# Both ends of the state-space scan: where the decay products and the low parts of the scaled inputs run, when the last transposes come, and where the first branch operands lie

## The chip, the cores and the metric

The kernel runs on one core of one Trainium2 chip. The metric is the device time of one execution in microseconds, the median of repeated runs. Before the change it is 2060.22 us (three runs, 2060.09 to 2060.29). A core has TensorE (PE: matmuls, with its weight loads, PEld, beside them), VectorE (DVE), ScalarE (ACT), GpSimd (POOL) and the SyncE queue (SP), which here issues nearly all DMAs. Matmul results land in PSUM banks and are copied out by ScalarE or VectorE; operands lie in the on-chip memory SBUF.

## The reference

One layer of a hybrid encoder on 1024 frames of width 1024, in float32. Three mixers (latent attention, forgetting attention, a chunked state-space scan) read one input projection; their outputs are gated and merged, and a feed-forward block follows. What matters here is the scan and the merge:

```python
def ssd_scan(x, dt, A, Bm, Cm):
    ...
    a_cum = jnp.cumsum(dtc * A.astype(jnp.float32).reshape(G, Hg), axis=2)
    xdt = xf * dtc[..., None]
    ...
    decay = jnp.where(causal, jnp.exp(jnp.where(causal, seg, 0.0)), 0.0)
    cb = jnp.einsum('bcign,bcjgn->bcijg', Cc, Bc)
    y_diag = jnp.einsum('bcijg,bcijgh,bcjghp->bcighp', cb, decay, xdt)
    decay_to_end = jnp.exp(a_cum[:, :, -1:] - a_cum)
    states = jnp.einsum('bcjgn,bcjgh,bcjghp->bcghpn', Bc, decay_to_end, xdt)
    chunk_decay = jnp.exp(a_cum[:, :, -1])

    def step(h, inp):
        st, dec = inp
        return h * dec[..., None, None] + st, h
    ...
    y_off = jnp.einsum('bcign,bcghpn,bcigh->bcighp', Cc, h_in, jnp.exp(a_cum))
    return (y_diag + y_off).reshape(Bsz, L, H, P).astype(x.dtype)
...
        y_b = fox_branch(u_fox, fox_q_gain[l], fox_k_gain[l], fox_b_f[l]) @ w_br_fox[l]
...
        g = jax.nn.sigmoid(u_gate + b_gate[l]).reshape(Bsz, S, N_BRANCH, D_MODEL)
        merged = g[:, :, 0] * y_a + g[:, :, 1] * y_b + g[:, :, 2] * y_c
```

## The kernel before

Every float32 matmul is made of three on a reduced-precision type: an operand is **split** into a high part (a ScalarE copy) and a low part (a VectorE subtraction of the high part from the source), and high x high, high x low and low x high are summed (`mm3`, line 190; `split`, lines 136 and 137).

The stages run one after the other: input projection, attention of both kinds, scan, branch products with the gated merge, output product, feed-forward block. Projection blocks that nobody needs at once, twelve for the convolution and 24 for the gates (`all_fill`, matmuls at line 1153), are a **fill**: a generator that hands TensorE a few matmuls at a time between the work of attention and scan. In the scan one **step** of it is 12 matmuls of 512 columns; two steps make half a block, four a block. What follows a block (the tanh of a gate half at line 1160, the store of the gate to DRAM at line 1167, the split of the next weights at lines 1103 and 1104) is put in a queue with a due time on a running clock of estimated TensorE work (`later`, `run_until`).

The scan works on chunks of 128 rows, eight of them. Three generators serve a chunk, each one round after the other:

- `ssd_a` (round c): eight transposes of x in two groups into the one bank "tp" (lines 1484, 1485); then transposes of B and the products of B with C in the same bank (1493, 1495), the mask product cbm (1497), xd = x dt (1501) and its split into the two halves of xdt (136, 137), xdd and the skip term y on GpSimd (1504, 1506); then four times a decay matrix: a matmul "pse" into one of three "py" banks (1511), two ScalarE passes, the mask product, and a split into Eh and El.
- `ssd_b` (round c + 1): the states "pst" in one of two "st" banks (1534), the decayed state hst = previous hst x cdec (1539) plus pst (1540); four groups of output matmuls "py" (1548, 1549), each in a "py" bank which two VectorE additions into y free (1551, 1552); after the second group the product "pof" with the incoming state (1561 to 1564). At the end y is multiplied with silu of z (1567), Square on ScalarE sums its squares (1570) with the tile yT as a place for the squares nobody reads, GpSimd and VectorE take the inverse root in some ten small instructions, and ScalarE scales y (1575).
- `ssd_c` (round c + 2): eight transposes of y in two groups into "tp" (1583), copied to yT (1584), stored to ys_d in DRAM (1586).

The order on TensorE is that of the program in this stage. It is made by `merge`: of the streams of a round, always the one least far along (its cost so far over its estimate, from a start offset) is advanced to its next yield; the fill is a stream of its own with a budget per round (`FILL_SSD`). A stream that yields 0.0 lets the least advanced other stream go once. On the other engines a scheduler orders the instructions by estimated times. One that is pinned (`pin`, from line 1092 on `keep_in_program_order`) cannot go ahead of the instruction that the program has just before it on its engine; in this stage these are the splits of the gate weights and what follows a convolution block.

After round 9 the rest of the fill is run out and the branch stage starts: for forgetting attention, latent attention and the scan in turn, the branch outputs are loaded from DRAM (line 1626) into the four shared buffers "t4", split into ah and al (slots of one pool, eight each), and multiplied with the branch weights (loaded and split in `load_w`, line 1043); the result times the gate (loaded at 1645) goes into `merged` (1652). The memory of this stage lies where the scan's tiles lay; a tile waits until the tiles on whose place it lies have been read for the last time.

Of the kernel before, what the change touches and what calls it, by code (L numbers as in the profile page):

```python
# [21 lines left out]
P = 128  # L22
D = 1024
# [19 lines left out]
def block_kernel(ctx: ExitStack, tc: tile.TileContext, x, positions, norm_mix_g, w_in, b_gate,  # L43
# [85 lines left out]
    def uid(s):  # L129
        cnt[0] += 1  # L130
        return f"{s}_{cnt[0]}"
# [909 lines left out]
    def load_w(pool, src, nk=NK, he=None, le=None):  # L1041
        raw = pool.tile([P, nk, P], F32, name=uid("wr"), tag="wr")
        SY.dma_start(raw, src)
        h = pool.tile([P, nk, P], F32R, name=uid("wh"), tag="wh")
        l = pool.tile([P, nk, P], F32R, name=uid("wl"), tag="wl")
        split(h, l, raw, he, le)
        return h, l
# [87 lines left out]

    def all_fill():
# [5 lines left out]
        for n, (kind, j, c0) in enumerate(blocks):  # L1142
# [5 lines left out]
            for half in range(2):  # L1148
# [8 lines left out]
                if kind == "c":  # L1157
                    fn = lambda ps=ps, hs=hs, u=u: A.activation(u[:, hs], ps, AF.Copy)
                else:
                    fn = lambda ps=ps, hs=hs, u=u, r=8 * kind + j: A.activation(  # L1160
                        u[:, hs], ps, AF.Tanh, bias=pc_g[:, r:r + 1], scale=0.5)
                pl[0] = later(1.4, fn)
                if half == 1:
                    if kind == "c":
                        conv_done(j, u, ul, 2.2)
                    else:
                        ul[0] = later(2.0, lambda u=u, g=g_d[kind][j]: SY.dma_start(g, u))
# [268 lines left out]

    with ExitStack() as ps__:
# [37 lines left out]
        def ssd_a(o, c):  # L1475
# [5 lines left out]
            for g in range(2):  # L1481
# [4 lines left out]
                yield 0.44  # L1486
            if c + 1 < NT:
                load_xs(obj[c + 1], c + 1)
# [13 lines left out]
            split(o.xdt[:, :, 0:64], o.xdt[:, :, 64:128], xd)  # L1502
# [6 lines left out]
            for q in range(4):  # L1509
# [11 lines left out]
                o.E.append((Eh, El))  # L1521
                yield 0.3

        def ssd_b(o, c, prev):
# [4 lines left out]
            if c + 1 < NT:  # L1529
                o.hst = pool.tile([P, 16, 64], F32, name=uid("hst"), tag="hst")  # L1530
                for g in range(2):
# [6 lines left out]
                    else:  # L1538
                        V.tensor_mul(o.hst[:, hs, :], prev.hst[:, hs, :], hb(cdec, c, hs))
# [30 lines left out]
            A.activation(o.yT.rearrange("p j s -> p (j s)"), yf, AF.Square, accum_out=ss)  # L1570
# [4 lines left out]
            A.activation(yf, yf, AF.Copy, scale=r)  # L1575

        def ssd_c(o, c):

            yf = o.y.rearrange("p h d -> p (h d)")
            for g in range(2):  # L1580
# [4 lines left out]
                yield 0.44  # L1585
            SY.dma_start(ys_d[:, :, c * P:c * P + P].rearrange("j p s -> p j s"), o.yT)

        with tc.manual_schedule(engines={mybir.EngineType.PE}):
# [8 lines left out]
            for c in range(NT + 2):  # L1597
# [3 lines left out]
                if 0 <= c - 2 < NT:  # L1601
                    st.append((ssd_c(obj[c - 2], c - 2), 0.88, 0.6 if c <= NT else 0.9))
# [9 lines left out]
    with ExitStack() as pe_:  # L1612
        wsp = pe_.enter_context(TP("wsp", 1, side="right"))
        mgs = [pe_.enter_context(TP(f"mg{i}", 1)) for i in range(4)]
        mp_ = pe_.enter_context(TP("mgp", 1))
# [4 lines left out]
        run_until(clk[0] + 100.0)  # L1620
        mh, ml = alloc_hn()
        for b, wsrc, nk in ((1, w_br_fox, 4), (0, w_br_mla, 4), (2, w_br_ssm, 8)):
            ah, al = [], []
            for k in range(nk):
                raw = fpl.tile([P, S], F32, name=uid("ar"), tag="t4", bufs=4)
                SY.dma_start(raw, ys_d[k] if b == 2 else att_d[b][k * P:k * P + P, :])
                h = mp_.tile([P, S], F32R, name=uid("ah"), tag="ah", bufs=8)
                l = mp_.tile([P, S], F32R, name=uid("al"), tag="al", bufs=8)
# [4 lines left out]
                else:  # L1633
                    split(h, l, raw)
# [3 lines left out]
            for j in range(NK):  # L1638
                if (b, j) in ((0, 2), (0, 6), (2, 1), (2, 3), (2, 5)):
                    down_sums([wsp.tile([P, 2, 512], F32, name=uid("ws"), tag=f"ws{i}") for i in range(4)])  # L1640
                elif (b, j) == (2, 6):
                    down_flush()
                wh, wl = load_w(fpl, wv[:, :, j * P:j * P + P], nk)
                g = fpl.tile([P, S], F32, name=uid("gl"), tag="t4", bufs=4)
                SY.dma_start(g, g_d[b][j])
                for half in range(2):
# [9 lines left out]
                    if b == 2:  # L1656
# [4 lines left out]
                        if j == NK - 1 and half == 0:  # L1661
                            last = (i0, i1)
    psg.close()
# [68 lines left out]

    def behind_(ins, other):
        tc.add_manual_dep(ins.ins, other.ins.name,
                          mybir.DependencyInfo(mybir.DependencyClass.NoSync, mybir.DependencyReason.DATA),
                          reason="behind")
        return ins
# [408 lines left out]
```

## Time and profile before

| | us |
|---|---|
| median of the runs shown | 2060.22 |
| the profiled execution's own time | 2058.1 |
| its span, first to last instruction | 2056.4 |
| busy in the span: PE / DVE / ACT / POOL | 2017.6 / 1381.7 / 936.7 / 655.4 |
| scan stage in it, about | 919 to 1141 |
| branch stage in it, about | 1141 to 1321 |

How to read the rows: a list of waits gives engine and line, the engine and line waited for, the microseconds in total, the number of times, and the longest. A timeline row gives the start, the busy time, engine, line, operation, out <- in, partitions and shapes, the number of instructions merged into it, and in brackets the idle time ahead of it and what ended it. A window row gives the stretch, its length, busy time and number of instructions of PE, PEld, DVE, ACT and POOL, then the granted TensorE clock (1.00 is full), the share of the DMA engines, and GB/s. Ends of matmuls are modelled: a matmul's row reaches past the start of the next.

### The profile page before, as it was taken

Reading aid. Unit: us, or ns where it says so; the run is one execution under the profiler, and the core shown is the slowest. Engines: PE = TensorE matmul, PEld = TensorE weight load, DVE = VectorE, ACT = ScalarE, POOL = GpSimd, SP = SyncE. Lnnn points to the kernel's source line nnn. Section 1 sums busy time; section 2 is a strip of 40 time slices with the busy share of each in tenths; the row PEclk is TensorE's granted clock in tenths of the full one; section 3 lists DMA queues with packets and bytes.
Section 4 is the critical chain, followed back from the end, with each engine's and each line's share of the span. In section 5 each row is a group of like instructions: output and inputs, shape, how many; then the busy total and the mean of one; then the engine's idle time right before and its main releaser. Section 6 shows DMA issues by size and latency. Waiting matters only on the chain. (4 is left out here: it accounts for less than half of the span.)

```text
span 2056.4 us, 28859 instructions
## 1 busy us (share of the span) xinstructions
PE 2017.6 (98%) x10253; PEld 1681.5 (82%) x10253; DVE 1381.7 (67%) x2410; ACT 936.7 (46%) x1700; POOL 655.4 (32%) x638
## 2 busy tenths in 40 slices
PE   9999999999999999999999999999999999999999
PEld 8999888888888888887777787888778888888887
DVE  7777566366566766656776357557987777675655
ACT  5555323255454655545565223323545445454432
POOL 5033212122221322223332063000464454523765
PEclk9999999999999999999999999999999999999999
DMA  6266848343444545424433679432422211239575
GB/s 174 66 198 213 282 136 255 109 130 116 126 111 122 131 108 150 113 77 119 129 120 96 211 243 321 152 123 77 131 87 86 92 52 41 92 128 335 199 258 187
DMA packets 276315, 303.09 MB, mean 147 GB/s; under 512 B 19101, under 2 KB 209577, under 8 KB 276170
## 3 DMA queue, kind: packets, MB, share of 16 engines
q1 hardware_dynamic: 276168, 301.24, 46.9%
q8 instruction: 81, 1.33, 0.3%
q14 instruction: 64, 0.52, 0.1%
q10 hardware_dynamic: 2, 0.00, 0.0%
HBM read 208.51 MB, written 92.67 MB: 146 GB/s over the span
## 5 line engine op out<-in xcount | busy, mean ns | idle before, releaser
L1297 POOL TENSOR_SCALAR pm<-pm,rs 128x128 f32<-128x128 f32 (+7 forms) x128 | 107.1, 840 | 426.7 <-DVE rs L1296 320.7
L1153 PE MATMUL mm<-hnh,wh 128*128 128x512 f32 x576 | 240.2, 417 | 0.0
L1153 PE MATMUL mm<-hnh,wl 128*128 128x512 f32 x576 | 226.6, 393 | 0.0
L1153 PE MATMUL mm<-hnl,wh 128*128 128x512 f32 x576 | 226.6, 393 | 0.0
L2093 PE MATMUL dn<-dr,dr 128*128 128x512 f32 x592 | 182.3, 389 | 0.0
L1290 ACT ACTIVATE pm<-s,nmx 128x128 f32<-128x128 f32 (+2 forms) x192 | 110.3, 581 | 71.3 <-DVE nmx L1287 61.3
L2093 PEld LDWEIGHTS dn<-dr,dr 128*128 128x128 f32 x592 | 111.1, 188 | 23.0
L1153 PEld LDWEIGHTS mm<-hnh,wl 128*128 128x128 f32 x576 | 108.6, 189 | 24.7
L1153 PEld LDWEIGHTS mm<-hnh,wh 128*128 128x128 f32 x576 | 109.4, 190 | 19.9 <-issue 4.4
L1153 PEld LDWEIGHTS mm<-hnl,wh 128*128 128x128 f32 x576 | 109.4, 190 | 15.9 <-issue 0.5
L1357 DVE TENSOR_TENSOR ptl<-tp,pth 128x512 fp32r<-128x512 f32 (+1 forms) x160 | 97.9, 631 | 34.0 <-ACT pth L1356 32.6
L2093 PE MATMUL dn<-dr 128*128 128x512 f32 x296 | 115.3, 389 | 1.1 <-DVE dY L2110 1.1
L1356 ACT ACTIVATE pth<-tp 128x512 fp32r<-128x512 f32 (+1 forms) x160 | 83.9, 555 | 69.3 <-PE tp L1351 69.2
L137 DVE TENSOR_TENSOR dr<-dr,dr 128x1024 fp32r<-128x1024 f32 x52 | 72.2, 1398 | 52.1 <-ACT dr L136 39.5
L190 PE MATMUL ybr<-ah,wh 128*128 128x512 f32 x256 | 100.1, 395 | 3.1 <-ACT ah L136 1.6
L190 PE MATMUL ybr<-al,wh 128*128 128x512 f32 x256 | 99.8, 392 | 0.2
L190 PE MATMUL ybr<-ah,wl 128*128 128x512 f32 x256 | 99.2, 390 | 0.0
L1285 DVE TENSOR_REDUCE nmx<-s 128x1 f32<-128x384 f32 (+3 forms) x128 | 65.9, 519 | 35.9 <-PE s L1284 34.5
L136 ACT ACTIVATE dr<-dr 128x1024 fp32r<-128x1024 f32 x52 | 54.9, 1063 | 72.9 <-PE dn L2093 51.2
L136 ACT ACTIVATE wh<-wr 128x1024 fp32r<-128x1024 f32 (+1 forms) x40 | 35.2, 879 | 101.3 <-PE ybr L190 53.1
L1351 PE MATMUL tp<-ident,pm 128*128 128x128 f32 x576 | 80.5, 275 | 0.0
L137 DVE TENSOR_TENSOR wl<-S,wh 128x1024 fp32r<-128x1024 f32 x42 | 63.2, 1504 | 23.5 <-ACT wh L136 23.5
(529 smaller groups left out, 5882.3 us busy)
## 6 DMA issues: line engine op xcount, KB each, us to landing
dr<-act_d SPq DMA_DIRECT2D x99, 256.0 KB
wr<-in_w_in_dram SPq DMA_DIRECT2D x36, 512.0 KB
g_d<-t SPq DMA_DIRECT2D x24, 512.0 KB
gl<-g_d SPq DMA_DIRECT2D x24, 512.0 KB
wr<-in_ffn_w_up_dram SPq DMA_DIRECT2D x23, 512.0 KB
ws<-in_ffn_w_down_dram SPq DMA_DIRECT2D x22, 512.0 KB
wsum_d<-ws SPq DMA_DIRECT2D x22, 512.0 KB
act_d<-fa SPq DMA_DIRECT2D x22, 512.0 KB
```

Source lines behind the costliest of these rows:

```text
L136: i = A.activation(h, src, AF.Copy) if he is A else he.tensor_copy(h, src)
L137: return i, le.tensor_sub(l, src, f32(h))
L190: T.matmul(ps, a(k), b(k), start=(i == 0), stop=(i == n - 1))
L1153: T.matmul(ps, a[:, k, :], b[half][:, k, :], start=(k == 0 and i == 0), stop=(k == NK - 1 and i == 2))
L1285: later(0.15, lambda: V.reduce_max(nmx[:, ci:ci + 1], ps[:, :b - a], axis=AX, negate=True))
L1290: pss[cj][1][0] = later(0.9 + 0.1 * cj, lambda cj=cj, a_=a_, b_=b_: A.activation(p_[:, a_:b_], pss[cj][0][:, :b_ - a_], AF.Exp, bias=nb, a ...
L1297: G.tensor_scalar(p_[:, 0:n * P], p_[:, 0:n * P], rs[:, 3:4], 0.0, op0=ALU.mult, op1=ALU.add)
L1351: T.transpose(pt[:, off:off + P], pn[qi][0][:, k * P:k * P + P], ident)
L1356: later(cs + 0.05, lambda th=th, pt=pt, off=off: A.activation(th[:, :off], pt[:, :off], AF.Copy))
L1357: pl[0] = later(cs + 0.6, lambda th=th, tl=tl, pt=pt, off=off: V.tensor_sub(tl[:, :off], pt[:, :off], f32(th[:, :off])))
L2093: T.matmul(ps[m], a[:, ts_], b[:, 512:], start=first_ and j == 0 and q == 0, stop=j == NFH - 1 and q == 2, skip_group_check=not first_)
```

## The change

Seven edits, all around the scan:

1. The decay product of `ssd_b` (line 1539) is pinned: it stays behind the VectorE instruction that the program has just before it.
2. The split of xd leaves its place behind xd: the high part is issued behind the first decay block of the round, the low part, pinned, behind the second.
3. `ssd_a` gets an empty yield between the second group of x transposes and the transposes of B; `ssd_c` one behind its first group, except in the last chunk.
4. Square writes to a scratch tile of its own, ysq (4 KB a partition), in place of yT.
5. In round 9 the stream of `ssd_c` gets cost 8.0 and offset 0.2 in place of 0.88 and 0.9. The tanh of the very last gate half and the store behind it are due 50 us later.
6. The first two fox outputs are loaded into a pool of their own, opened ahead of the scan on the other side of memory (two of the four scratch tiles of the down sums move there as well). The operand pairs of fox are four fixed pairs of tiles, high and low in turn, ahead of the others in memory.
7. On ScalarE, the high parts of fox's operands and of its first weight block are ordered behind the last scale of y (1575), and the last gate tanh and the second weight block behind the second high part.

```diff
+    def behind_(ins, other):
+        tc.add_manual_dep(ins.ins, other.ins.name,
+                          mybir.DependencyInfo(mybir.DependencyClass.NoSync, mybir.DependencyReason.DATA),
+                          reason="behind")
+        return ins
+
+    def load_w(pool, src, nk=NK, behind=None):
...
-        split(h, l, raw, he, le)
+        i, _ = split(h, l, raw)
+        if behind is not None:
+            behind_(i, behind)
...
+    def gate_tanh(o, i, b):
+        t = A.activation(o, i, AF.Tanh, bias=b, scale=0.5)
+        if gate_behind[0] is not None:
+            behind_(t, gate_behind[0])
...
-                pl[0] = later(1.4, fn)
+                wait = 50.0 if n == len(blocks) - 1 and half == 1 else 0.0
+                pl[0] = later(wait + 1.4, fn)
...
+    pfr = ExitStack()
+    frp = pfr.enter_context(TP("frp", 1, side="right"))
...
                 A.activation(xT[:, 512 * g:512 * g + 512], pt, AF.Copy)
                 yield 0.44
+            yield 0.0
...
             V.tensor_mul(xd, xv, hb(dt, c))
-            split(o.xdt[:, :, 0:64], o.xdt[:, :, 64:128], xd)
...
                 o.E.append((Eh, El))
+                if q == 0:
+                    A.activation(o.xdt[:, :, 0:64], xd, AF.Copy)
+                elif q == 1:
+                    pin(V.tensor_sub(o.xdt[:, :, 64:128], xd, f32(o.xdt[:, :, 0:64])))
                 yield 0.3
...
-                        V.tensor_mul(o.hst[:, hs, :], prev.hst[:, hs, :], hb(cdec, c, hs))
+                        pin(V.tensor_mul(o.hst[:, hs, :], prev.hst[:, hs, :], hb(cdec, c, hs)))
...
-            A.activation(o.yT.rearrange("p j s -> p (j s)"), yf, AF.Square, accum_out=ss)
+            sq = pool.tile([P, D], F32, name=uid("ysq"), tag="ysq", bufs=1)
+            A.activation(sq, yf, AF.Square, accum_out=ss)
...
-            A.activation(yf, yf, AF.Copy, scale=r)
+            scaled[0] = A.activation(yf, yf, AF.Copy, scale=r)
...
                 yield 0.44
+                if g == 0 and c + 1 < NT:
+                    yield 0.0
...
-                    st.append((ssd_c(obj[c - 2], c - 2), 0.88, 0.6 if c <= NT else 0.9))
+                    st.append((ssd_c(obj[c - 2], c - 2), *((0.88, 0.6) if c <= NT else (8.0, 0.2))))
...
-        mp_ = pe_.enter_context(TP("mgp", 1))
+        mps = [pe_.enter_context(TP(n, 1)) for n in ("mpf", "mpm")]
...
-        run_until(clk[0] + 100.0)
...
+        def ops_tile(i):
+            return [mps[i // 4].tile([P, S], F32R, name=uid(n), tag=f"{n}{i}") for n in ("ah", "al")]
...
+                if b == 1 and k < 2:
+                    raw = frp.tile([P, 2, 512], F32, name=uid("ar"), tag=f"ws{k}").rearrange("p a s -> p (a s)")
+                else:
+                    raw = fpl.tile([P, S], F32, name=uid("ar"), tag="t4", bufs=4)
...
-                    split(h, l, raw)
+                    e = split(h, l, raw)
+                    if b == 1:
+                        behind_(e[0], scaled[0])
+                        if k == 1:
+                            gate_behind[0] = e[0]
+                            run_until(clk[0] + 100.0)
...
-                wh, wl = load_w(fpl, wv[:, :, j * P:j * P + P], nk)
+                wh, wl = load_w(fpl, wv[:, :, j * P:j * P + P], nk, (scaled, gate_behind)[j][0] if b == 1 and j < 2 else None)
```

26 lines of the change are left out of this document (13 added, 13 removed).

## The prediction

> **What bounds the kernel now.** I read the page first, then TensorE's waits in the stretch that the diff touches, then the timeline of each engine around every wait, and last the windows with the granted clock.
>
> ```profile
> span 2056.4 us, 28859 instructions
> ...
> PE 2017.6 (98%) x10253; PEld 1681.5 (82%) x10253; DVE 1381.7 (67%) x2410; ACT 936.7 (46%) x1700; POOL 655.4 (32%) x638
> ```
>
> TensorE is the bound from end to end. The change adds and removes no matmul, so it can only win TensorE's idle time, and whatever slower clock follows an idle stretch. Between 905 and 1150 us, the scan and the head of the branch stage, these are all of its waits over 0.5 us but the one at the scan's door, which nothing in the diff reaches:
>
> ```profile
> PE py L1548 <- DVE y L1552: 2.9, 1, 2.9
> PE stp L1493 <- ACT xT L1485: 2.1, 3, 0.7
> PE ybr L190 <- ACT ah L136: 1.6, 1, 1.6
> PE stp L1583 <- ACT yT L1584: 1.1, 1, 1.1
> PE stp L1583 <- ACT y L1575: 1.1, 1, 1.1
> ```
>
> Together 8.8 us, in four places. The first and the third cost more than they show. TensorE's timeline after the 2.9, then the windows there and at the end:
>
> ```profile
> 950.35 0.32 PE L1548 MATMUL py<-xdt,Eh 128*128 128x128 f32 x1 [2.90 <-DVE y L1552]
> ...
> 953.36 0.63 PE L1153 MATMUL mm<-hnl,wh 128*128 128x512 f32 x1
> 953.79 0.63 PE L1153 MATMUL mm<-hnh,wl 128*128 128x512 f32 x1
> ...
> 957.20 0.44 PE L1153 MATMUL mm<-hnl,wh 128*128 128x512 f32 x1
> ```
> ```profile
> 948.00:954.00 6.00, 3.65 (x12) 2.99 (x13) 4.08 (x8) 2.36 (x5) 0.00 (x0) 0.71 0.01 1
> 954.00:960.00 6.00, 6.00 (x22) 4.30 (x22) 2.61 (x5) 3.34 (x7) 0.00 (x0) 0.72 0.11 40
> 960.00:966.00 6.00, 6.00 (x29) 4.89 (x28) 4.68 (x9) 4.81 (x9) 2.18 (x5) 1.00 0.75 228
> ...
> 1140.00:1146.00 6.00, 4.39 (x12) 3.55 (x13) 1.56 (x2) 3.44 (x4) 0.00 (x0) 0.72 0.99 291
> ```
>
> The granted clock (the figure after POOL's) is 0.71 and 0.72 behind those two stalls and 1.00 elsewhere. From 950.35 to 957.20 the 512-wide matmuls start 0.43 us apart; at full clock it is 0.23 (1137.37 to 1137.60 in the end's rows below). A slow stretch so loses 0.20/0.43 of its length: 6.85 x 0.47 = 3.2 us here. The start stall costs 2.9 + 3.2 = 6.1.
>
> **Part 1, the start.** Who is late for that matmul: it needs the third "py" bank, which VectorE frees with two additions. VectorE's rows, the last of an undisturbed xd product:
>
> ```profile
> 940.00 1.29 DVE L1537 COPY hst<-pst 128x512 f32<-128x512 f32 x2
> 941.20 3.02 DVE L1539 TENSOR_TENSOR hst<-hst,cdec 128x512 f32<-128x512 f32 x2
> 944.14 2.92 DVE L1501 TENSOR_TENSOR xd<-xT,dt 128x1024 f32<-128x1024 f32 x1
> ...
> 948.19 1.23 DVE L137 TENSOR_TENSOR xdt<-xd,xdt 128x1024 fp32r<-128x1024 f32 x1 [0.79 <-ACT xdt L136]
> ...
> 949.78 0.42 DVE L1552 TENSOR_TENSOR y<-y,py 128x256 f32<-128x256 f32 x1
> ...
> 969.59 1.23 DVE L1501 TENSOR_TENSOR xd<-xT,dt 128x1024 f32<-128x1024 f32 x1 [1.26 <-ACT xT L1485]
> ```
>
> Two things stand ahead of the additions and are not wanted yet: the decay products of chunk 1 (3.02), floated one round early, and the low part of xdt (0.79 wait and 1.23), which the next round's matmuls read. The pin sends the first back to its own round (two instructions of about 0.65, beside pst), behind the VectorE instruction issued just ahead of it in the program; the move sends the second behind the second exponential block. Then xd can start when the transposed x is there, about 941.7, and ends at 944.6 even at its disturbed 2.92; the small cbm product (0.41) and the first two additions (0.87) follow. The third py falls at about 946.3 in the new order of part 2 (from 940.39: four transposes 0.36, a gate step 2.7, B's 0.6, two py groups 0.9 each, one pse 0.4), with the first py done at 945.2, so the additions end about 946.1. That is tight: any 0.4 to 0.7 us instruction in the way shows. I take 5.8 of the 6.1; bounds 0 (still over 2 us late) and 6.1. What moves in elsewhere: 1.3 us of products at each round's start, against 1.2 to 2 us of low part leaving that place, on a VectorE that is busy 4.68 us of the window 960 to 966. That is the slower rival's ground.
>
> **Part 2, the empty yield.** I worked the rule of the merge (always the stream least far along) through both versions, with 44 gate steps of 12 matmuls left (the first of 6) and -0.1 us owed at the start, which reproduces the order of the trace in all ten rounds. In rounds 1, 4 and 7 nothing stands between the second x transposes and those of B, which wait for the one transpose bank:
>
> ```profile
> 940.39 0.60 PE L1484 MATMUL stp<-ident,t 128*128 128x128 f32 x4
> 941.68 0.44 PE L1493 MATMUL stp<-ident,bc 128*128 128x128 f32 x2 [0.69 <-ACT xT L1485]
> ```
>
> With the yield a gate step (2.7) or a py group (0.9) comes between in every round: 3 x 0.69 = 2.1 us. The cover is longer than the 0.69 it hides. B's transposes, and the mask product and exponentials behind them, come later by as much; their readers stand in the next round, over 6 us on. Bounds 0 and 2.1; taken 2.1.
>
> **Part 3, Square in its own tile.** In round 3 and at the end ScalarE's Square waits until the previous chunk's store has read yT:
>
> ```profile
> 989.80 1.06 ACT L1570 ACTIVATE yT<-y 128x1024 f32<-128x1024 f32 x1 [2.60 <-DMA ys_d<-yT]
> 1001.43 1.15 ACT L1575 ACTIVATE y<-y,yr 128x1024 f32<-128x1024 f32 x1 [4.03 <-POOL yr L182]
> ```
>
> The scale of the same chunk comes 11.6 us later, and the transposes at 1002.6 wait 1.1 us for it. 2.6 us earlier covers that: 1.1, bounds 0 and 1.1.
>
> **Part 4, the end.**
>
> ```profile
> 1120.65 0.48 PE L1153 MATMUL mm<-hnh,wh 128*128 128x512 f32 x1
> ...
> 1137.37 0.39 PE L1153 MATMUL mm<-hnh,wl 128*128 128x512 f32 x1
> 1137.60 0.60 PE L1583 MATMUL stp<-ident,y 128*128 128x128 f32 x4
> 1139.32 0.65 PE L1583 MATMUL stp<-ident,y 128*128 128x128 f32 x4 [1.12 <-ACT yT L1584]
> 1141.61 2.07 PE L190 MATMUL ybr<-ah,wh 128*128 128x512 f32 x4 [1.63 <-ACT ah L136]
> ...
> 1145.12 0.40 PE L190 MATMUL ybr<-ah,wl 128*128 128x512 f32 x1
> ```
> ```profile
> 1121.76 1.22 DVE L1567 SCALAR_TENSOR_TENSOR y<-y,t 128x1024 f32<-128x1024 f32 x1
> ...
> 1145.67 3.50 DVE L137 TENSOR_TENSOR al<-ar,ah 128x1024 fp32r<-128x1024 f32 x3 [2.86 <-DMA ys_d<-yT]
> ```
> ```profile
> 1124.77 0.36 SPq L1586 DMA_DIRECT2D ys_d<-yT  x1
> ...
> 1128.83 2.49 SPq L1626 DMA_DIRECT2D ar<-att_d  x3
> ```
> ```profile
> 1128.06 1.06 ACT L1570 ACTIVATE yT<-y 128x1024 f32<-128x1024 f32 x1 [0.16 <-DVE wl L137]
> ...
> 1132.42 1.15 ACT L1575 ACTIVATE y<-y,yr 128x1024 f32<-128x1024 f32 x1 [3.21 <-POOL yr L182]
> ...
> 1140.51 2.94 ACT L136 ACTIVATE ah<-ar 128x1024 fp32r<-128x1024 f32 x3
> ```
>
> Now the last transposes, their copies and the first fox split stand in a row with nothing beside them: 1.12 + 1.63 = 2.75 us idle, then a slow clock to 1145.12: 3.51 x 0.47 = 1.65. In the new order the six gate steps from 1120.65 (72 matmuls, 2.7 each) run: two, second transposes of chunk 6, two, first transposes of chunk 7, one, second transposes of chunk 7, one. The first transposes of chunk 7 thus fall near 1131.9. Is y scaled by then? Its product ends at 1122.98; Square then waits for the store issued at 1124.77 and for what is queued ahead, and the scale ends 5.5 us after Square starts (1128.06 to 1133.58). In its own tile Square can start at 1123, so the scale ends near 1128.6, 3.3 us before it is wanted. Behind it stand the two first fox high parts (about 1.0 each), then their low parts (1.23); 2 x 2.2 us fits ahead of the last gate step's end near 1138. Both copies of the transposes lie under the last two gate steps. The last tanh goes behind the second high part; nobody waits for it but its store. Six loads are touched: two raw loads leave SP's 1128.83 group for memory of their own, two keep the shared buffers, and two weight loads only have their splits ordered. The low part that waited 2.86 for the store lay on yT's place; by the sizes of the tiles the four fox pairs now lie below it, on xdt, xd, xdd and y, read out by then, save the fourth low part, which waits for chunk 7's transposes. Taken 4.4; bounds 0 and 4.4.
>
> **The sum.** 5.8 + 2.1 + 1.1 + 4.4 = 13.4. The idle figures count from a matmul's modelled end, 0.16 past the next one's start (0.39 long, 0.23 apart), so each of seven bridged stalls gives 0.15 more: 1.0. In all 14.4. Against the profiled span that is 2056.4 - 14.4 = 2042.0, against that execution's own 2058.1 it is 2043.7, and against the median of the runs shown, 2060.2, it is **2045.8**. In the rest of the branch stage, to 1330, TensorE's longest wait is
>
> ```profile
> PE ybr L190 <- ACT ah L1630: 1.2, 1, 1.2
> ```
>
> so that stage has no slack in which the gain could drown, and behind it TensorE stays the bound.
>
> [...]
>
> **The rivals.**
> - Start stall stays (0.10): VectorE runs another floating instruction ahead of the additions, which no pin forbids. For it: the 0.2 us margin. Gives back 5.8 and 0.2: 2051.8.
> - The end turns into a new wait (0.13): Square does not come forward, because ScalarE's order puts a weight copy that waits for TensorE ahead of it; the scale then ends at 1133.6, and TensorE stands 1.7 us at 1131.9 and hardly less ahead of ybr. Against it: those copies are now ordered behind the scale. About 3 us less: 2049.
> - The slow stretches are no consequence of the stalls (0.04): 3.2 + 1.65 stay: 2050.6. The rows speak against it, both standing directly behind a stall.
> - No effect (0.04): VectorE is late in any order, or the two halves cancel: 2060.
> - **Slower (0.09):** the VectorE instruction just ahead of the pinned decay products is, from round 2 on, the second seed of the previous chunk's inverse root, which waits for Square and GpSimd:
>
> ```profile
> 991.26 0.15 DVE L175 TENSOR_SCALAR rg_i<-yv 128x1 int32<-128x1 int32 x1 [3.29 <-POOL yv L1572]
> ```
>
>   The products, the additions of pst that free the "st" banks, and whatever else VectorE has queued then stand behind that wait, and TensorE at pof in each of rounds 2 to 7. A stall like the one at 950 costs 6.1; two leave a gain, from the third it is slower, six give 2060.2 - 14.4 + 36.6 = 2082. Against it: pof follows pst by two py groups and at least one gate step, some 5 us, against 2.6 us for products and additions, and Square comes earlier where it was held up.
>
> **How the numbers follow.** The forecast has 0.60. Below 2043.5 nothing is left to win but the scan's door. Up to 2053 the range holds the first three rivals: about 0.82 in all after the edges of each. What cannot be told from no change is 0.2%, 4.1 us. Faster: 0.60 + 0.10 + 0.13 + 0.04 = 0.87; same 0.04; slower 0.09.
>
> **What would show it.** Right: no 2.9 us wait at py L1548 and a clock of 1.00 around it; the decay products in 2 x 0.65 beside pst from round 2 on; no wait of B's transposes for xT; Square with no wait for ys_d; both last transposes before the last gate matmuls, and ybr directly behind these at full clock. Wrong: a wait at py, pof or the y transposes that was not there, above all one longer than 2 us with slow matmuls behind it.

## The result, and the profile after

The changed kernel takes 2047.38 us (median of 6 executions, 2045.54 to 2048.7) beside 2060.2 us of the kernel before on the same chip (6 executions); ratio 0.9938, 95% interval 0.9925 to 0.9951. The profiled execution took 2045.89 us, its span is 2044.2, 12.2 less than before. The forecast was 2045.8, with 14.4 less.

The page of the changed kernel, its first lines:

```profile
span 2044.2 us, 28874 instructions
...
PE 2013.8 (99%) x10253; PEld 1678.3 (82%) x10253; DVE 1387.1 (68%) x2410; ACT 936.4 (46%) x1700; POOL 652.9 (32%) x638
```

TensorE's waits in the changed kernel, as far as they belong to the scan and the branch stage (engine and line, what was waited for, us in total, times, longest):

```profile
PE stp L1502 <- DVE o L1349: 0.9, 1, 0.9
...
PE ybr L190 <- ACT ah L1665: 0.7, 1, 0.7
PE ybr L190 <- DVE al L1666: 0.7, 1, 0.7
PE stp L1502 <- ACT yT L1607: 0.6, 2, 0.3
...
PE stp L1606 <- ACT y L1598: 0.2, 1, 0.2
```

None of the five waits that the prediction listed is left in its size: the 2.9 of the third output group, the three of 0.69 and the 1.6 ahead of ybr are gone, and of the waits of the y transposes 0.2 is left. The 0.9 is the one at the scan's door. The two rows of ybr stand far behind the head of the branch stage, at 1222 and 1226 us, where the scan's own outputs come in; before waits 1.2 us at that place. Now the stretch in which the 2.9 stood, first as windows (length, then busy time and number for PE, PEld, DVE, ACT, POOL, then the granted clock), then as TensorE's timeline:

```profile
942.00:948.00 6.00, 6.00 (x41) 5.25 (x39) 3.47 (x8) 2.49 (x4) 4.88 (x2) 0.98 0.34 88
948.00:954.00 6.00, 6.00 (x14) 3.94 (x14) 4.36 (x7) 2.56 (x5) 0.00 (x0) 0.50 0.02 3
954.00:960.00 6.00, 6.00 (x29) 4.64 (x30) 3.88 (x7) 4.69 (x8) 0.00 (x0) 0.95 0.43 146
```
```profile
944.46 0.31 PE L1570 MATMUL py<-xdt,Eh 128*128 128x128 f32 x1
...
947.76 0.79 PE L1529 MATMUL pse<-segr,segl 10*128 10x512 f32 x1
948.49 0.80 PE L1168 MATMUL mm<-hnh,wh 128*128 128x512 f32 x1
...
953.90 0.79 PE L1529 MATMUL pse<-segr,segl 10*128 10x512 f32 x1
954.62 0.33 PE L1570 MATMUL py<-xdt,Eh 128*128 128x128 f32 x1
```

TensorE is busy for all of the 18 us, there is no stall, and still the clock is 0.50 from 947.76 to 954.62. This is the surprise of the result: the stall went and the half clock behind it stayed, 6.86 us long as before (6.85). At the end of the scan it did go. The same views there, and ScalarE's timeline:

```profile
1128.00:1134.00 6.00, 6.00 (x30) 4.91 (x29) 2.36 (x2) 3.85 (x5) 0.00 (x0) 1.00 0.75 274
```
```profile
1126.03 0.60 PE L1606 MATMUL stp<-ident,y 128*128 128x128 f32 x4
1129.24 0.60 PE L1606 MATMUL stp<-ident,y 128*128 128x128 f32 x4
1132.45 0.62 PE L190 MATMUL ybr<-ah,wh 128*128 128x512 f32 x2
```
```profile
1116.89 1.06 ACT L1593 ACTIVATE ysq<-y 128x1024 f32<-128x1024 f32 x1 [2.39 <-DVE y L1589]
...
1121.35 1.15 ACT L1598 ACTIVATE y<-y,yr 128x1024 f32<-128x1024 f32 x1
...
1130.37 2.00 ACT L136 ACTIVATE ah<-ar 128x1024 fp32r<-128x1024 f32 x2
```

Square waits for its product and no longer for a store; the scale ends at 1122.5, 3.5 us ahead of the first of the last transposes; both groups of these have gate matmuls behind them, and the first branch matmul follows the last gate matmul without a gap.

### The profile page after: what moved, and what is told of

The parts are those of the page before. It is cut to its first block, busy times and chain, and to the rows that moved or that the text cites. A ratio compares the mean times of both kernels' runs of the same rounds, so it can differ in the third digit from the quotient of the medians.

```text
span 2044.2 us, 28874 instructions
## 1 busy us (share of the span) xinstructions
PE 2013.8 (99%) x10253; PEld 1678.3 (82%) x10253; DVE 1387.1 (68%) x2410; ACT 936.4 (46%) x1700; POOL 652.9 (32%) x638
```

## Where the 12.2 us come from

The two timelines give three lengths: from the first x transposes (919.30 before, 920.01 after) to the first branch matmul (1141.61, 1132.45), from there to the last branch matmul, and the rest.

| | before | after | won |
|---|---|---|---|
| ahead of the scan | 919.30 | 920.01 | -0.7 |
| scan, first x transposes to first ybr | 222.31 | 212.44 | 9.9 |
| branch matmuls | 178.52 | 176.82 | 1.7 |
| the rest of the span | 736.3 | 734.9 | 1.3 |

The first row lies outside of the diff, and of the last row the diff touches only where two scratch tiles lie. Both move from profile to profile where no edit reaches: in the fourteen profiles of this study the scan begins anywhere between 919.30 and 927.01, and in the thirteen of the changed kernel and its variants the rest goes from 734.4 to 736.4, so that before's 736.3 lies within. That is more than most of the edits are worth, so below a kernel is judged by the length of its scan and by the waits in it, beside its median.

| kernel | median us | ratio to before, 95% | scan us | half-clock windows in it |
|---|---|---|---|---|
| before | | | 222.31 | 2 |
| after | 2047.38 | 0.9925 to 0.9951 | 212.44 | 2 |
| again | 2046.55 | 0.9924 to 0.9952 | 210.88 | 1 |
| broken_run | 2045.46 | 0.9917 to 0.9945 | 211.17 | 1 |
| second_run | 2049.02 | 0.9934 to 0.9969 | 210.07 | 0 |
| fine_steps | 2047.52 | 0.9928 to 0.9957 | 211.34 | 0 |
| fine_round1 | 2046.33 | 0.9924 to 0.9951 | 209.33 | 0 |
| no_pin | 2051.45 | 0.9939 to 0.9974 | 214.67 | 2 |
| low_part_early | 2047.34 | 0.9925 to 0.9958 | 213.35 | 2 |
| no_yield | 2049.35 | 0.9935 to 0.9969 | 214.08 | 1 |
| square_yT | 2054.99 | 0.9970 to 0.9991 | 218.02 | 2 |
| late_transposes | 2051.65 | 0.9946 to 0.9974 | 213.58 | 1 |
| free_order | 2053.01 | 0.9953 to 0.9977 | 211.47 | 0 |
| old_memory | 2046.30 | 0.9925 to 0.9953 | 209.30 | 0 |

A half-clock window is explained next. All kernels but before are the changed kernel with the edit shown. From again on they ran in three groups, each on a chip of its own beside executions of before, whose medians were 2059.37, 2060.03 and 2059.82; so medians of different groups can be compared to within about 0.7 us.

## Experiments on the clock

**again**: no edit.

> The changed kernel itself, timed again beside the three below. Theory 'light windows': the clock of TensorE is decided window by window, each about 3.4 us long, on a grid that is not tied to the program, and a window with little matmul work in it (idle, or 128-column matmuls with fresh weights) halves it for the next one or two. Then the three groups of output matmuls in a row in round 1 are hit in some executions and missed in others: mean clocks between 0.998 and 1.000, spans that differ by 1.6 to 3.4 us between them, median near 2047. Rival 'the place': the clock falls whenever the scan starts; every execution shows 0.998 and they lie within 1 us.

Its six executions have mean clocks from 0.998 to 1.000, spans from 2042.2 to 2046.8 and a median of 2046.55. "The place" falls. In its profile the clock is halved only from 950.8 to 954.2, in a scan of 210.88 us; in the changed kernel's first profile it was halved for twice as long, in a scan of 212.44. The instructions are the same, and nothing in round 1 waits in either.

**Where half clock begins.** The windows of 0.2 us in which it sets in, of before, of broken_run and of second_run:

```profile
544.20:544.40 0.20, 0.00 (x0) 0.00 (x0) 0.20 (x2) 0.00 (x0) 0.00 (x0) 0.73 0.58 205
950.40:950.60 0.20, 0.20 (x2) 0.20 (x3) 0.17 (x2) 0.00 (x0) 0.00 (x0) 0.70 0.00 0
1141.60:1141.80 0.20, 0.20 (x1) 0.20 (x2) 0.20 (x1) 0.20 (x1) 0.00 (x0) 0.56 1.08 328
```
```profile
545.80:546.00 0.20, 0.20 (x4) 0.20 (x3) 0.20 (x2) 0.20 (x1) 0.00 (x0) 0.75 1.15 266
955.40:955.60 0.20, 0.20 (x3) 0.15 (x2) 0.20 (x2) 0.20 (x1) 0.00 (x0) 0.75 0.00 0
```
```profile
39.80:40.00 0.20, 0.20 (x3) 0.20 (x2) 0.20 (x2) 0.20 (x2) 0.15 (x1) 0.51 0.96 389
821.40:821.60 0.20, 0.20 (x3) 0.20 (x3) 0.20 (x2) 0.00 (x0) 0.00 (x0) 0.64 1.00 410
```

A mean of 0.73 over 0.2 us that begin at 1.00 and end at 0.50 puts the edge at 0.46 of the way, 544.29. So the edges lie at 544.29, 950.48 and 1141.62 in before, at 545.90 and 955.50 in broken_run, at 39.80 and 821.46 in second_run. Their distances, 406.19, 191.14, 409.60 and 781.66, are 119, 56, 120 and 229 times 3.4133, each within 0.02 us. The unit is measured: the clock record of before's trace has half-clock stretches of 3.413, 6.827 and 3.413 us, that of the changed kernel one of 6.827 (the 6.86 above is counted between starts of matmuls), and the four distances divided by their counts give 3.4132 to 3.4134. Every half-clock stretch of these profiles that the end of the span doesn't cut is one or two such lengths long. So in these profiles half clock begins on a grid of 3.413 us which the program's start doesn't place: counted back by 159 lengths, an edge lies at 1.6 us of before's span (544.29 - 542.7) and at 3.2 of broken_run's (545.90 - 542.7). A length of the grid at half clock costs 1.6 us: 212.44 (two) - 210.88 (one).

What comes ahead of the edges at the scan's start is a length of the grid in which TensorE does little. In the changed kernel it is 944.35 to 947.76: B's last products, three output groups and a decay matmul, without any wait. The output groups bring 192 columns in 0.22 us, where the gate matmuls bring 512 in 0.23; by that the window holds about two fifths of the columns of a gate window (an estimate from these spacings). In before it is 947.07 to 950.48, of which the stall takes 2.9.

So in the changed kernel a length that was busy throughout, with narrow matmuls, was enough for half clock: PE busy 3.41 of the 3.41 us from 944.35 to 947.76, then 0.50 in the window from 948 to 954 above.

**broken_run** moves one gate step of round 1 ahead of the third output group:

```diff
-    FILL_SSD = [11.3] * 8 + [12.0, 24.5]
+    FILL_SSD = [11.3, 11.9, 10.7] + [11.3] * 5 + [12.0, 24.5]
```

> One gate step is moved ahead of the third output group of round 1, so that no three output groups stand in a row there. 'Light windows': no clock under 0.98 between 935 and 965, mean clock 0.999 to 1.000 in nearly every execution, about 2 us less than 'again' in the median and up to 3.2 less where that one was hit. 'The place': a slow stretch of 3.4 or 6.8 us stays at the scan's start, time within 0.5 us of 'again'.

A miss in the profile: half clock from 955.50 on, for one length of the grid. The gate step ends at 951.44, and from there to 954.96 come the third output group, two decay matmuls, the fourth group and another decay matmul, with 0.45 us of wait for an exponential. The light stretch was cut at one place and made at the next, and half clock moved with it. The mean clock of its six executions is 0.9995 beside 0.9986 of the changed kernel's twelve, and the medians are not told apart.

**second_run** gives round 4 the order of round 1:

```diff
-                if q == 1 and prev is not None:
+                if q == (3 if c == 3 else 1) and prev is not None:
```

> The product with the incoming state of chunk 3 comes after the fourth output group in place of after the second, so that round 4 has the order of round 1: B's transposes, two output groups, a decay matmul, the third output group, a decay matmul, a gate step. 'Light windows': a second slow stretch of 3.4 or 6.8 us near 1015 to 1035 in a good part of the executions, mean clocks down to 0.996, median 1 to 3 us above 'again'. 'The place': no slow clock there, time within 0.7 us of 'again' (the banks of the moved product may cost some tenths).

Its profile shows neither: no half clock in the scan at all, though now two rounds have the three groups. The edges of its grid, counted on from 821.46, fall at 1016.02, 1019.43 and 1022.84; the light stretch of round 4, from 1016.74 to 1021.46, lies across the middle one, and neither side was light enough, a wait of 0.33 us for an exponential included. Other executions do pay, by their clocks: two of its six have a mean clock of 0.996, where none of the changed kernel's twelve is under 0.998, and the median is 2.5 us over again's, though the intervals overlap. That a light stretch is hit only by chance is what sets "light windows" apart from "the place".

**fine_steps** halves the gate steps of rounds 0 to 7:

```diff
             for c in range(NT + 2):
+                grain[0] = 2 if c < NT else 4
                 st = []
```

> In rounds 0 to 7 the gate steps are 6 matmuls long in place of 12, twice as many, so that no stretch of about 3.4 us of the scan is without gate matmuls; the work is the same. 'Light windows' (the clock falls after a window of 3.41 us, on a grid free of the program, in which little is multiplied): no clock under 0.9 between 925 and 1130, mean clock 0.999 to 1.000, 2 to 3 us under 'again' in the median where no new wait eats it (the banks of the output groups and the exponentials have half as much cover at each place: waits of 0.3 to 0.7 us may come). If the slow clock had another cause: the slow stretch near 950 stays and the median is within 1 us of 'again'.

No half clock and no wait in the scan:

```profile
923.01:1134.35 211.34, 211.34 (x1043) 160.23 (x1043) 152.92 (x248) 126.37 (x202) 61.95 (x80) 1.00 0.40 124
```

Yet it takes 211.34 us. The timeline has 73 stretches of gate matmuls in the scan where the changed kernel has 41, and the first matmul of a stretch stands 0.31 to 0.34 us ahead of the second, not 0.23. Added up over the rows of both, the thirty-two more such starts cost about 2.5 us, as an estimate, and the small waits that vanished give back 0.8; measured are 2.1 us over the changed kernel's scan less its two half-clock windows (209.2). What the full clock won went into the finer steps. One profile at full clock doesn't show that it was won by them: second_run, free_order and old_memory have no half clock in the scan either. The five executions have a mean clock of 0.9990, little over the 0.9986 of the changed kernel. How light its windows are says more, and is told in the last section.

**fine_round1** does the same in round 1 alone, with the budgets set so that the other rounds keep their order:

```diff
-    FILL_SSD = [11.3] * 8 + [12.0, 24.5]
+    FILL_SSD = [11.3, 12.6, 10.0] + [11.3] * 5 + [12.0, 24.5]
...
             for c in range(NT + 2):
+                grain[0] = 2 if c == 1 else 4
                 st = []
```

> Gate steps of 6 matmuls in round 1 alone, with the budget of rounds 1 and 2 set so that the order of all other rounds is that of the changed kernel. 'Light windows': no clock under 0.9 between 925 and 965; from the first x transposes to the first branch matmul about 209.7 us (the 210.1 to 212.4 of the kernels with that order of round 1, less their slow windows of 1.6 us each, and some 0.4 for the extra switches between small and wide matmuls); median 1 to 1.5 us under 'again'. Rival, what the finer steps cost is not the switches but waits of their own: that stretch is 211 us or more, median no better than 'again'.

```profile
921.24:1130.57 209.33, 208.55 (x1043) 160.74 (x1043) 155.21 (x248) 125.84 (x202) 63.79 (x80) 1.00 0.41 125
```

The scan is as long as hoped, 209.33, at full clock, and the profile's span of 2042.0 is the shortest of the fourteen. The median, 2046.33, does not show the 1 to 1.5 us: what varies ahead of the scan is larger. The mean clock of its five executions is 0.9992. It is the best version here by its trace, and not shown to be faster than the changed kernel.

## Experiments on the parts

**no_pin** and **low_part_early** undo one half of the start each:

```diff
-                        pin(V.tensor_mul(o.hst[:, hs, :], prev.hst[:, hs, :], hb(cdec, c, hs)))
+                        V.tensor_mul(o.hst[:, hs, :], prev.hst[:, hs, :], hb(cdec, c, hs))
```

> The decay products are not pinned; the low part stays where the change put it. Both delays needed (3.0 us of early decay products and 2.0 of low part with its wait, against a stall of 2.9): the products float one round early again, xd starts about 2.4 us later than in the changed kernel, and TensorE waits about 0.9 us (0.5 to 1.5) for the additions at the third output group of round 1; 0.5 to 1.5 us slower. Rival, the low part alone was the delay: no wait there over 0.3 us, time the same. Second rival, the pin alone carries it: a wait of 2 us or more.

```diff
             V.tensor_mul(xd, xv, hb(dt, c))
+            split(o.xdt[:, :, 0:64], o.xdt[:, :, 64:128], xd)
...
-                if q == 0:
-                    A.activation(o.xdt[:, :, 0:64], xd, AF.Copy)
-                elif q == 1:
-                    pin(V.tensor_sub(o.xdt[:, :, 64:128], xd, f32(o.xdt[:, :, 0:64])))
```

> The split of xd stands behind xd again; the decay products stay pinned. Both delays needed: the additions come about 2.0 us later than in the changed kernel and TensorE waits about 0.5 us (0.2 to 1.0) for them at the third output group of round 1. Rival, the decay products alone were the delay: no wait over 0.2 us. Second rival, the low part carries it: a wait of 2 us or more. In the other rounds nothing over 0.3 us in any of the three cases.

VectorE and then TensorE without the pin, and the same with the low part early:

```profile
945.89 2.95 DVE L1520 TENSOR_TENSOR xd<-xT,dt 128x1024 f32<-128x1024 f32 x1
948.76 2.99 DVE L1561 TENSOR_TENSOR hst<-hst,cdec 128x512 f32<-128x512 f32 x2
...
952.01 0.40 DVE L1573 TENSOR_TENSOR y<-y,py 128x256 f32<-128x256 f32 x1
```
```profile
953.01 0.45 PE L1570 MATMUL py<-xdt,Eh 128*128 128x128 f32 x1 [2.37 <-DVE y L1574]
```
```profile
946.79 0.73 DVE L1570 TENSOR_TENSOR y<-y,py 128x256 f32<-128x256 f32 x2
947.45 0.73 DVE L1571 TENSOR_TENSOR y<-y,py 128x256 f32<-128x256 f32 x2
```
```profile
948.11 0.33 PE L1567 MATMUL py<-xdt,Eh 128*128 128x128 f32 x1 [0.75 <-ACT E L1535]
```

Without the pin the products run one round early again, behind xd this time, and the stall is 2.37. That is the size which the second rival gave, the pin alone carrying it, and not the 0.9 of the theory. But 1.73 of it is xd itself: it takes 2.95 beside GpSimd here and 1.22 in the changed kernel (last section). With xd at 1.22 some 0.6 would be left, an estimate, within the 0.5 to 1.5 of the theory.

With the low part early, another wait of 0.75 comes at the same place, for an exponential. The additions are late as well: the second addition into y of the first group begins at 947.45, while TensorE has been free for the third group since 947.36. So each edit undone alone brings a wait back, 2.37 and 0.75, and the pin is the larger part; how much of the 0.75 the additions alone would have cost isn't shown.

**no_yield**:

```diff
                 yield 0.44
-            yield 0.0
```

> The empty yield ahead of B's transposes is taken out, the rest of the change stays. If the yield's gain is what it covers: three waits of 0.69 us of B's transposes for the copy of x in rounds 1, 4 and 7, 2.1 to 2.4 us in all, and the median 2 to 3 us above 'again'. Rival, the idle time only moves: the waits come back but others, at the output groups or the exponentials, go, and the idle time of the scan grows by less than 1 us.

```profile
PE stp L1511 <- ACT xT L1503: 2.1, 3, 0.7
```

The three waits are back in rounds 1, 4 and 7, nothing else went for them, and the scan less its one half-clock window is 212.5, 3.2 over the 209.3 of old_memory: the rival falls.

**square_yT**:

```diff
-            sq = pool.tile([P, D], F32, name=uid("ysq"), tag="ysq", bufs=1)
-            A.activation(sq, yf, AF.Square, accum_out=ss)
+            A.activation(o.yT.rearrange("p j s -> p (j s)"), yf, AF.Square, accum_out=ss)
```

> Square writes to yT again, the rest of the change stays. By the prediction: Square waits for the store of ys_d in one or two rounds (2 to 3 us) and the scale and the transposes behind it come late: 1.1 us on TensorE at the second y transposes, and at the end, where the scale has 3.5 us to spare, up to 2 us more if Square waits there too; 1 to 3 us slower. Rival, with the new order of the y transposes the wait of Square is hidden: no wait of the y transposes over 0.3 us, time the same.

ScalarE and TensorE at the end of the scan:

```profile
1123.68 1.06 ACT L1592 ACTIVATE yT<-y 128x1024 f32<-128x1024 f32 x1 [4.81 <-DMA ys_d<-yT]
...
1128.03 1.15 ACT L1597 ACTIVATE y<-y,yr 128x1024 f32<-128x1024 f32 x1 [2.63 <-POOL yr L182]
```
```profile
1129.23 1.11 PE L1605 MATMUL stp<-ident,y 128*128 128x128 f32 x4 [5.65 <-ACT y L1597]
```

The direction was right and the size was not: the last transposes, moved ahead, stand 5.65 us for a scale that Square made late, and two half-clock windows follow. This is the largest loss of the study, 8.7 us of scan over old_memory's 209.3. In round 3 the wait is 0.59, not 1.1.

**late_transposes**:

```diff
-                    st.append((ssd_c(obj[c - 2], c - 2), *((0.88, 0.6) if c <= NT else (8.0, 0.2))))
+                    st.append((ssd_c(obj[c - 2], c - 2), *(0.88, 0.6 if c <= NT else 0.9)))
```

> The stream of the last transposes gets its old cost and offset back, everything else of the change stays. If the end's gain is the cover of these transposes by gate matmuls: the two waits of 1.1 and 1.0 to 1.6 us come back between the last gate matmuls and the first branch matmul, 2 to 2.8 us, and with a slow clock behind them up to 4.4; median 2 to 4.4 above 'again'. Rival: the early operands and their order carry the end; then TensorE waits only for the last copy of the transposes or not at all, and the median is within 0.7 us of 'again'.

```profile
1134.68 0.66 PE L1606 MATMUL stp<-ident,y 128*128 128x128 f32 x4 [0.74 <-ACT yT L1607]
1136.97 0.73 PE L190 MATMUL ybr<-ah,wh 128*128 128x512 f32 x2 [1.63 <-ACT ah L136]
1138.23 0.50 PE L190 MATMUL ybr<-al,wh 128*128 128x512 f32 x1 [0.53 <-DVE al L137]
```

Both waits are back, with a third for the low part; the scan less its half-clock window is 212.0, 2.7 over old_memory's. Its median is 5.1 over again's, above the 4.4 expected: the branch matmuls take 179.25 us in place of 176.6, through waits for weights and operands split too late (1.0 for wl, and 1.2 for al where the changed kernel has 0.7, among them).

**free_order** and **old_memory** undo the order and the memory of the first operands:

```diff
-                    if b == 1:
-                        behind_(e[0], scaled[0])
-                        if k == 1:
-                            gate_behind[0] = e[0]
-                            run_until(clk[0] + 100.0)
+                    if b == 1 and k == 1:
+                        run_until(clk[0] + 100.0)
...
-                wh, wl = load_w(fpl, wv[:, :, j * P:j * P + P], nk, (scaled, gate_behind)[j][0] if b == 1 and j < 2 else None)
+                wh, wl = load_w(fpl, wv[:, :, j * P:j * P + P], nk)
```

> The order on ScalarE of the first branch operands is left to the scheduler (the high parts and weight copies are not put behind the last scale, the last gate tanh and the second weights not behind the second high part); the transposes and the memory stay as changed. If the order carries part of the end: the high part of the first operand or of the first weights comes after a copy that waits for TensorE, the first branch matmul waits 0.5 to 2 us, 0.5 to 3 us slower. Rival, only the transposes' place and the memory matter: no wait over 0.3 us ahead of the first branch matmul, time the same.

```diff
-                if b == 1 and k < 2:
-                    raw = frp.tile([P, 2, 512], F32, name=uid("ar"), tag=f"ws{k}").rearrange("p a s -> p (a s)")
-                else:
-                    raw = fpl.tile([P, S], F32, name=uid("ar"), tag="t4", bufs=4)
+                raw = fpl.tile([P, S], F32, name=uid("ar"), tag="t4", bufs=4)
...
-                if b == 1:
-                    h, l = fox_hl[k]
-                else:
-                    h, l = ops_tile(4 + k if b == 0 else k)
+                h = mp_.tile([P, S], F32R, name=uid("ah"), tag="ah", bufs=8)
+                l = mp_.tile([P, S], F32R, name=uid("al"), tag="al", bufs=8)
```

> The first branch operands are loaded into the shared buffers and split into the one pool of before; the order on ScalarE and the place of the transposes stay as changed. If the memory of their own counts: the first two loads wait until the shared buffers are free and a low part for the store of ys_d on yT's place, TensorE waits 1 to 3 us ahead of or behind the first branch matmul, 1 to 4 us slower. Rival: the loads come in time anyway, no new wait over 0.5 us.

ScalarE and TensorE with the free order, then VectorE and TensorE with the old memory:

```profile
1136.28 0.63 ACT L136 ACTIVATE wh<-wr 128x512 fp32r<-128x512 f32 x1 [1.95 <-PE mm L1168]
1136.82 0.67 ACT L1147 ACTIVATE t<-mm,pc_g 128x512 f32<-128x512 f32 x1
1137.38 3.89 ACT L136 ACTIVATE ah<-ar 128x1024 fp32r<-128x1024 f32 x4
```
```profile
1138.48 2.01 PE L190 MATMUL ybr<-ah,wh 128*128 128x512 f32 x4 [2.01 <-ACT ah L136]
```
```profile
1133.56 2.36 DVE L137 TENSOR_TENSOR al<-ar,ah 128x1024 fp32r<-128x1024 f32 x2 [1.91 <-DMA ys_d<-yT]
```
```profile
1134.84 0.50 PE L190 MATMUL ybr<-al,wh 128*128 128x512 f32 x1 [1.40 <-DVE al L137]
```

Left to the scheduler, the first high part stands behind a weight copy, ahead of which ScalarE stood 1.95 us for the gate matmuls, and behind the last gate tanh: 2.01 us ahead of ybr, a half-clock window behind it, and branch matmuls of 178.41 us. Scan and branch matmuls together take 389.9 us, 3.8 more than in fine_round1; the median is 6.5 over again's, and what the rest of that is was not followed up. In the old memory a low part waits for the last store again, and TensorE 1.40 us for it. That wait stands behind the first ybr, so the scan's length doesn't hold it: scan and branch matmuls together take 387.5 us, 1.4 more than in fine_round1, which has no half clock there either. By the trace the memory so is worth about 1.4 us; the median is again's and does not show it.

## Why the prediction came out as it did

**The idle time: right.** 2.9 + 2.1 + 1.1 + 2.75 + 1.0 for the modelled ends make 9.85. Before's 222.31 us of scan less that, and less the two half-clock windows of the start (3.2), is 209.3; the scans without half clock measure 209.30 (old_memory) and 209.33 (fine_round1). The order of TensorE and the places of the waits came out as forecast in parts 2 and 4.

**The start: the step that failed.** "The start stall costs 2.9 + 3.2 = 6.1", of which 5.8 was taken, put the half clock down to the stall that stood ahead of it. Only the 2.9 came. Two windows stayed in the profile, one in again's, none in second_run's, all with the same order of round 1 and no wait for the additions there. In the prediction's own rows the one follows the other, and in before the length ahead of the edge does hold the stall. What the step left out is what fills that length once the stall is gone: three output groups and a decay matmul, little enough work for the clock to fall again where the grid lay so, as in this profile and in again's. The 3.2 was counted as all but sure and is a matter of chance. Within this part, "two things stand ahead of the additions" held, with unlike sizes: a wait of 2.37 comes back without the pin, 0.75 with the low part early.

**The number.** That the forecast of 2045.8 is within 1.6 us of the median is in part luck. In the profile, scan and branch matmuls won 11.6 of the 14.4; the other 0.6 of its 12.2 comes from stretches that the diff doesn't work on, and the same kernel in again has one half-clock window where this execution had two.

**The end: right**, 2.75 us of idle and one half-clock window, 1.65 forecast and 1.7 won in the branch matmuls. But the margin of 3.3 us, which was 3.5, hangs on Square's own tile: without it the moved transposes wait 5.65. **Part 3** put 1.1 on that edit, from round 3; as a condition of part 4 it is worth 5.65 and two half-clock windows more.

**The rivals.** That the half clock is no consequence of the stalls, given 0.04, was half right: at the start it stayed, at the end it went. The new wait at the end did not come; square_yT shows its place and its price. The slower rival's row is there, the decay products behind the two seeds of the inverse root and a weight split:

```profile
962.51 0.15 DVE L175 TENSOR_SCALAR rg_i<-yv 128x1 int32<-128x1 int32 x1 [2.01 <-POOL yv L1595]
...
962.78 1.23 DVE L1112 TENSOR_TENSOR wl<-wr,wh 128x1024 fp32r<-128x1024 f32 x1
963.92 0.68 DVE L1561 TENSOR_TENSOR hst<-hst,cdec 128x512 f32<-128x512 f32 x1
```

VectorE stands 2.01 us there, but no wait of TensorE for pof or pst is in the list: the cover of some 5 us held.

**The clock over many executions.** A half-clock window lowers the mean clock by 1.71 / 2050 = 0.0008. The 38 executions of before that ran beside the twelve experiments have a mean of 0.9961, the twelve of the changed kernel 0.9986; that is 4.7 windows against 1.7, and three windows are 4.8 us, as an estimate (each clock is given to 0.001). These windows are counted over the whole span, not in the scan alone. The prediction's 3.2 + 1.65 was about the size of this gain on the average, though not of what its profile lost.

## What to carry to other kernels

Price a stall by its idle time first; here the half clock behind it, 1.6 us for each length, came behind a whole grid length of 3.413 us with little work in it, and a row of narrow matmuls made such a length (944.35 to 947.76 in the changed kernel) as well as a stall did (2.9 us of 947.07 to 950.48 in before). So look for light stretches, not only for waits, and for the same program hit in one execution and spared in the next, as in again's six with mean clocks from 0.998 to 1.000; compare a stage's own length and the mean clocks, not one span. Before moving an instruction earlier, find what makes its operand late: here a borrowed scratch tile decided whether the move won 4.4 us or lost more.

## What the runs showed of the hardware

The clock's grid, with its 3.4133 us and 1.6 us for each half-clock length, is told above. A count over TensorE's rows of all fourteen traces bears the light windows out, as an estimate. Cut at each profile's own edges, the scan and what follows it to 1146 us have some 900 lengths of 3.413 us that begin at full clock. Let each matmul count with its columns, weighted by the share of 128 rows that it uses, so that a decay matmul with its 10 rows counts for little; a length of gate matmuls then has about 7600. Half clock follows eleven of these lengths. Ten of them are among the eleven lightest of all, at most 2510; the eleventh, ahead of the half clock in free_order, has 2760. In kernels with the changed kernel's round 1 at full clock, the lightest stretch of 3.413 us in that round has about 2110, old_memory's for one; in fine_round1 and fine_steps it has over 3800, wherever the edges lie. So by this count the finer steps did take the light window of round 1 away, and the kernels at full clock without them were spared by the place of the grid.

Which measure of work decides stays open all the same, as the weights were chosen afterwards: late_transposes has 0.74 and 1.63 us of idle within 3 us of each other, 2230 by this count in the first of the two lengths, and no half clock behind them.

Where xd on VectorE and xdd on GpSimd began together, one of the two took longer. GpSimd beside the xd of no_pin, then both in the changed kernel, then GpSimd in before:

```profile
945.85 1.91 POOL L1522 TENSOR_TENSOR xdd<-xT,dend 128x1024 f32<-128x1024 f32 x1 [13.91 <-ACT xT L1503]
```
```profile
942.03 3.02 POOL L1522 TENSOR_TENSOR xdd<-xT,dend 128x1024 f32<-128x1024 f32 x1 [13.92 <-ACT xT L1503]
```
```profile
942.07 1.22 DVE L1520 TENSOR_TENSOR xd<-xT,dt 128x1024 f32<-128x1024 f32 x1
```
```profile
941.77 1.91 POOL L1504 TENSOR_TENSOR xdd<-xT,dend 128x1024 f32<-128x1024 f32 x1 [14.36 <-ACT xT L1485]
943.63 2.35 POOL L1506 TENSOR_TENSOR y<-xT,Db 128x1024 f32<-128x1024 f32 x1
```

One of xd and xdd takes its own time (1.91 on GpSimd, 1.22 on VectorE, which are also the medians of the eight of each in the changed kernel), and the other takes about both times, 2.95 or 3.02. Which of them that is can't be read from the starts: GpSimd's row begins 0.04 ahead of VectorE's in both kernels. The 3.02 and 2.92 us of VectorE that the prediction read as work or a disturbance lie beside GpSimd's two products of before, from 941.77 to 945.98. In the changed kernel the decay products take 0.68 and 0.70 in round 2 and xd 1.22; by that some 1.6 of the 3.02 and 1.7 of the 2.92 came from running beside GpSimd, as an estimate. No bracket in the timeline remarks on it, and by what the two engines hold each other up isn't shown. The 2.37 of no_pin holds such a delay too, the 1.73 of xd.
